# A two-layer GLA and differential-attention trunk: channel-major activations, contiguous weight tiles, and one head of the next unit ahead of an out-projection

## The chip, the cores and the metric

The kernel runs on one core of one Trainium2 chip. A core has a matmul engine (TensorE, "PE" in the profile, with its weight loads as "PEld"), a vector engine (VectorE, "DVE"), an activation engine (ScalarE, "ACT"), GpSimd ("POOL") and a queue that issues DMAs (SyncE, "SP"). The metric is the device time of one execution in microseconds, lower is better; the time given is the median of several executions.

## The reference

The reference runs two layers over a sequence of 2048 tokens with 1024 channels, all in float32:

```python
for l in range(2):
    mod = silu(c) @ w_ada[l] + b_ada[l]              # c: 1 x 1024
    shift, scale, gate = split(mod, 3)
    h = rms_norm(x, norm_g[l]) * (1 + scale) + shift
    proj = h @ w_in[l]                               # 1024 -> 3600 columns
    gq, gk, gv, glr, gz, dq, dk, dv, dz = split(proj)
    gq, gk, gv = silu(causal_conv4([gq, gk, gv]))    # then gated linear attention, 4 heads, chunks of 64
    o_gla  = rms_norm(gla(gq, gk, gv, glr)) * silu(gz)
    o_diff = rms_norm(softmax1 @ dv - lam * softmax2 @ dv) * silu(dz)   # 4 heads, block-causal in chunks of 64
    x = x + gate * ([o_gla, o_diff] @ w_out[l])
```

`rms_norm` divides each token by the root of its mean square over channels. The result is `x` after the second layer.

## The kernel before

**Tiling.** The sequence is cut into four units of 512 tokens; with two layers there are eight units, which I number 0 to 7 (0 to 3 are layer 0). A unit's normalised input h is held channel-major, as eight tiles k of 128 channels by 512 tokens, each twice: `hhi` is h rounded to the matmul's fast float32 form, `hlo` the remainder. A weight tile is split likewise, into `hi` and `lo`. A product then takes three matmuls of 512 moving columns (hi·hi, lo·hi, hi·lo), accumulated over the eight k in one PSUM bank.

**Items of a unit.** The input projection is done as seven items of 512 columns: items 0 to 3 are the attention heads (each with the head's q, k, v and z), items 4 and 5 are the columns of the gated linear attention (GLA), item 6 is its output gate gz. An item has 96 matmuls (8 k, 4 banks, 3 products). The out-projection (`out_gen`) has two halves of 96 matmuls. An item occupies four PSUM banks of the pool `acc`; the other four banks (`tp`, `sc`, `po`) serve everything else. In the profile's names, `acc<-w,hhi` and `acc<-w,hlo` are the matmuls of the heads and of the gate (token-major result), `acc<-hhi,w` those of the GLA items (channel-major result), `acc<-w,oh` and `acc<-w,ol` those of the out-projection (oh, ol are the two parts of its input, four k from GLA and four from the heads).

**Making h.** For layer 0, unit 0 this is `start()`; otherwise `prep_gen`. `load_x` (line 703) loads 128 tokens by 1024 channels as `xt`, takes the sum of squares on ACT, the root on POOL, and scales the tile on DVE. `make_h` (line 719) turns it channel-major on PE: 8 transposes of 128x128 for each 128 tokens, 32 in a unit (`sc<-ident,xt`, `tp<-ident,xt`), then ACT applies the scale and shift out of PSUM and writes `hhi`, and DVE writes `hlo`. The buffers of `hhi` and `hlo` are single, so tile k of the next unit can only be written when the last matmul of the current unit (item 6) has read tile k.

**Modulation.** In layer 0, shift and scale come from `ada_load` and `ada_first` (lines 573 and 580): 8 MB of w_ada are loaded and multiplied on PE (`tp<-wr,cact`, then `sc<-sel,t`). The gate of the residual is computed in `ada_part` part 2, broadcast over tokens by a matmul with ones, and multiplied into the raw w_out tiles on DVE (line 679) before these are split.

**Weights.** `weights` (line 667) loads a raw tile on first use, splits it on ACT and DVE, and writes the split tile to DRAM (`wd`); later units load the split tile. For item 0 of layer 0 the split is done in units 0 and 1 and kept in unit 1 only.

**Order of the work.** Streams of generators (projections, attention, GLA, preparation, modulation) are merged by a list of due times; each operation is recorded, and a planner (`Program.order`, `best_order`, lines 215 and 248) lists the operations with its own costs and fixes each engine's order before the kernel runs. On the chip every engine goes through its list in order and waits where an operand isn't there. `dense_stream` (line 1317) is the stream of the projections: for each unit it waits for h, then takes the out-projection of the unit before, then the unit's items. The exception is the first unit of layer 1, where two heads come ahead of the out-projection:

```python
ahead = 2 if l and u == 0 else 0
if ahead:
    yield from dense_gen(l, u, items[:ahead])
if prev:
    yield from out_gen(*prev)
yield from dense_gen(l, u, items[ahead:])
```

All DMAs are issued by SP, in its list's order.

## Time and profile before

| | |
|---|---|
| time, median of 3 runs | 2454.96 us (2453.43 to 2455.94) |
| the profiled execution's own time | 2454.26 us |
| its span, first to last instruction | 2452.5 us |
| PE busy | 2403.7 us (98%), 13251 matmul records |
| DVE busy | 1778.8 us (73%) |
| ACT busy | 1283.8 us (52%) |
| DMA, share of 16 engines | 71.5%, 568.33 MB |
| granted PE clock | 1.000 |

The span is 1.8 us shorter than the execution's own time, and that time lies 0.7 us under the median. A busy time is the union of the instructions' spans; a matmul's span includes its pipeline, so that the next one starts before it ends, and the distance from start to start is what a matmul costs in a row of them. A float32 matmul that isn't in the fast form is two records in the trace. Almost all instructions are recorded by one helper and so share line 372; groups are told apart by the names of their tiles.

### The profile page before, as it was taken

How to read it: one execution, taken by the hardware profiler on the slowest of the kernel's cores; microseconds unless marked ns; L12 is line 12 of the kernel's file. 1: busy time of each engine (PE TensorE's matmuls, PEld its weight loads, DVE VectorE, ACT ScalarE, POOL GpSimd, SP SyncE). 2: the span in 40 equal slices, each digit the busy share in tenths (PEclk: the TensorE clock that was granted, in tenths of full speed). 3: DMA queues.
4: the chain of work that ended last, by engine and by line, in shares of the span. 5: the costliest groups of instructions: out<-in, count | busy, mean ns of one | idle time of the engine just before them, and what ended most of it. 6: DMA issues, size and time to landing. Idle time of an engine off the chain costs nothing. (4 is left out here: it accounts for less than half of the span.)

```text
span 2452.5 us, 39647 instructions
## 1 busy us (share of the span) xinstructions
PE 2403.7 (98%) x13251; PEld 1957.3 (80%) x13251; DVE 1778.8 (73%) x5169; ACT 1283.8 (52%) x2912; POOL 138.2 (6%) x424
## 2 busy tenths in 40 slices
PE   8999999999999999999999999999999999999998
PEld 5887778888888877888788777888788887878887
DVE  4879778882879828889764894778648877288983
ACT  5757545572555624455863573455624556145442
POOL 0101000010000000000000010000000000000000
PEclk9999999999999999999999999999999999999999
DMA  9778988667786776778467867676667776677663
GB/s 275 274 252 281 328 260 252 216 234 235 224 253 190 256 230 189 220 216 248 140 221 262 298 246 271 212 235 202 212 234 224 232 232 215 223 223 225 196 200 131
DMA packets 425997, 568.33 MB, mean 232 GB/s; under 512 B 195968, under 2 KB 300608, under 8 KB 425792
## 3 DMA queue, kind: packets, MB, share of 16 engines
q1 hardware_dynamic: 425792, 565.79, 71.5%
q8 instruction: 105, 1.72, 0.3%
q14 instruction: 100, 0.82, 0.1%
HBM read 410.52 MB, written 161.48 MB: 233 GB/s over the span
## 5 line engine op out<-in xcount | busy, mean ns | idle before, releaser
L372 PE MATMUL acc<-w,hhi 128*128 128x512 f32 x2560 | 835.0, 400 | 3.7 <-DVE z L372 1.2
L372 PEld LDWEIGHTS acc<-w,hhi 128*128 128x128 f32 x2560 | 467.8, 188 | 97.9 <-ACT ub L372 3.9
L372 PE MATMUL acc<-w,hlo 128*128 128x512 f32 x1280 | 505.9, 396 | 0.0
L372 ACT ACTIVATE s<-s,mx 128x128 f32<-128x128 f32 (+15 forms) x256 | 308.2, 1204 | 263.3 <-DVE s L372 151.2
L372 PE MATMUL acc<-hhi,w 128*128 128x512 f32 x1024 | 353.6, 399 | 0.0
L372 PE MATMUL acc<-w,oh 128*128 128x512 f32 x1024 | 334.0, 399 | 4.7 <-DVE t L372 2.2
L372 DVE TENSOR_SCALAR_CACHE_REDUCE s<-sc,mx 64x64 f32<-64x64 f32 (+5 forms) x640 | 306.4, 483 | 37.5 <-PE sc L372 18.2
L372 PEld LDWEIGHTS acc<-w,hlo 128*128 128x128 f32 x1280 | 240.7, 188 | 48.8 <-issue 0.8
L372 PEld LDWEIGHTS acc<-w,oh 128*128 128x128 f32 x1024 | 188.9, 188 | 46.1 <-DVE t L372 5.2
L372 PEld LDWEIGHTS acc<-hhi,w 128*128 128x128 f32 x1024 | 191.8, 188 | 38.5 <-DMA w<-wd 0.7
L372 PEld LDWEIGHTS po<-Vj,s 128*128 128x128 f32 x1536 | 193.4, 196 | 12.4 <-DMA s<-ad 5.7
L372 PE MATMUL po<-Vj,s 128*128 128x128 f32 x1536 | 198.9, 281 | 3.7 <-DMA s<-ad 2.5
L372 PE MATMUL acc<-w,ol 128*128 128x512 f32 x512 | 201.5, 396 | 0.0
L372 PE MATMUL acc<-hlo,w 128*128 128x512 f32 x512 | 201.0, 393 | 0.0
L372 DVE SCALAR_TENSOR_TENSOR s<-s,r 128x512 f32<-128x512 f32 (+2 forms) x320 | 198.4, 667 | 2.6
L372 DVE TENSOR_SCALAR_CACHE_REDUCE s<-sc 128x512 f32<-128x512 f32 (+4 forms) x256 | 157.8, 620 | 39.9 <-PE sc L372 31.5
L372 ACT COPY rw<-acc 128x256 f32<-128x256 f32 x128 | 48.4, 378 | 252.7 <-PE acc L372 252.1
L372 PE MATMUL sc<-Kj,qh 128*128 128x512 f32 x384 | 160.3, 417 | 4.1 <-DVE z L372 2.2
L372 POOL MEMSET s<- 64x64 f32 x256 | 37.2, 145 | 2086.1 <-PE po L372 1505.5
L372 DVE TENSOR_TENSOR w<-raw,w 128x512 fp32r<-128x512 f32 x152 | 103.3, 686 | 67.7 <-ACT w L372 67.0
L372 PE MATMUL sc<-Kj,ql 128*128 128x512 f32 x384 | 151.7, 395 | 0.0
L372 ACT CAST w<-raw 128x512 fp32r<-128x512 f32 x152 | 93.3, 628 | 102.9 <-PE acc L372 90.6
(185 smaller groups left out, 3738.6 us busy)
## 6 DMA issues: line engine op xcount, KB each, us to landing
w<-wd SPq DMA_DIRECT2D x424, 512.0 KB, 4.6
wd<-w SPq DMA_DIRECT2D x144, 512.0 KB, 4.0
raw<-in_w_in_dram SPq DMA_DIRECT2D x120, 256.0 KB, 4.7
Kj<-kd SPq DMA_DIRECT2D x48, 512.0 KB, 5.8
ad<-s SPq DMA_DIRECT2D x24, 768.0 KB, 5.3
s<-ad SPq DMA_DIRECT2D x24, 768.0 KB, 7.4
wr<-in_w_ada_dram SPq DMA_DIRECT2D x128, 128.0 KB, 3.0
ad<-s SPq DMA_DIRECT2D x32, 512.0 KB, 3.7
```

Source lines behind the costliest of these rows:

```text
L372: getattr(self.engines[e], method)(*[real(a) for a in args], **{k: real(v) for k, v in kw.items()})
```

## The change

**Layouts.** The host hands the arrays over in other layouts: x channel-major per unit (`xl`: unit, 128 channels of a tile, 8 tiles, 512 tokens) and also as it was; the nine weight items of each layer as contiguous tiles of two k each (`w_all`); the columns for glr, the small vectors, the lambdas and w_gk each in one array; the shift and scale columns of layer 0's w_ada transposed (`w_mod`). The result is written channel-major and turned on the host; the intermediate x (`XD`) is channel-major too.

**h.** `make_h` now takes a channel-major x tile: DVE multiplies it by the channel's scale and by the tokens' reciprocal roots (broadcast over partitions, `rsb`), ACT adds the shift and writes `hhi`, DVE writes `hlo`. There is no transpose of x. The reciprocal roots go through a small DRAM row (`RD`) and are broadcast by a DMA. Their sums of squares come, for units 1 to 3, from a second load of x token-major (ACT); for layer 1 from squares added up in `out_gen` (ACT and DVE) and four matmuls with a ones column (`sc<-ones,sqs`); for unit 0 in the same way inside `start()`.

**Start.** `start()` computes shift and scale of layer 0 per k on DVE (`wm<-wm,cb` with an accumulated sum) and no longer on PE. Items 0 and 4 of unit 0 run together: for each k, as soon as h of that k is there, both items' matmuls of that k, in the four `acc` banks and in the four other banks. The raw tiles of item 4 are therefore, like those of item 0, split twice (units 0 and 1) and kept in unit 1.

**Out-projection.** Weights are the stationary and oh, ol the moving operand, so that the result is channel-major; the gate is one scalar per channel and is applied when the bank is added to x (`scalar_tensor_tensor` in place of `tensor_tensor`). The multiplication of raw w_out by the gate goes.

**Order.** In all units but the first of layer 1, the first item (head 0) of a unit is put ahead of the previous unit's out-projection (`ahead` is 1 instead of 0); unit 0 takes the same item order as the others.

```diff
-    def make_h(l, xs, pr, kk):
+    def make_h(l, k, xk, rsb):
         y = layers[l]
-        ps = tp() if kk % 2 else sc()
-        for j in range(2):
-            k = 2 * kk + j
-            for i in range(2):
-                T.transpose(ps[:, j * 256 + i * P:j * 256 + i * P + P], xs[i][:, k * P:(k + 1) * P], ident)
...
+        hi, lo = state["hhi"][k], state["hlo"][k]
+        V.scalar_tensor_tensor(xk, xk, y.A[:, k:k + 1], rsb, op0=ALU.mult, op1=ALU.mult)
+        A.activation(hi, xk, AF.Identity, bias=y.B[:, k:k + 1])
+        V.scalar_tensor_tensor(lo, xk, y.B[:, k:k + 1], hi.bitcast(F32), op0=ALU.add, op1=ALU.subtract)
+
+    def add_square(sqs, xk, first):
+        if first:
+            A.activation(sqs, xk, AF.Square)
+        else:
+            sq = t2()
+            A.activation(sq, xk, AF.Square)
+            V.tensor_tensor(sqs, sq, sqs, op=ALU.add)
+
+    def sum_squares(sqs):
+        ps = sc()
+        for t in range(TT):
+            T.matmul(ps[:, 2 * t:2 * t + 1], sqs[:, t * P:(t + 1) * P], ones[:, 0:1], start=True, stop=True)
+        return ps[:, 0:2 * TT].rearrange("p (t o) -> p t o", o=2)[:, :, 0]
...
     def prep_gen(l, u, xsrc):
         key = l * NU + u
+        if l == 0:
+            yield need("h", key - 1, lag=6.0)
+            ss = p_sm.tile([P, TT], F32, tag="xss", name="xss", bufs=2)
+            for t in range(TT):
+                xt = p_q.tile([P, D], F32, tag="q", name="xt")
+                SY.dma_start(xt, x[u * UT + t * P:u * UT + (t + 1) * P, :])
+                A.activation(xt, xt, AF.Square, accum_out=ss[:, t:t + 1])
+                yield pe(0, 2.0)
+            rs_write(key, root(ss))
+        rsb = rs_tile()
+        SY.dma_start(rsb, RD[key].broadcast_to([P, UT]))
         yield need("free_h", key)
...
+        for c in range(KT // 2):
+            xp = p_q.tile([P, 2, UT], F32, tag="q", name="xp")
+            SY.dma_start(xp, xsrc(u)[:, 2 * c:2 * c + 2, :])
+            for j in range(2):
+                make_h(l, 2 * c + j, xp[:, j, :], rsb)
...
     def start():
...
+        for k in range(KT):
...
+            for part in range(2):
+                V.scalar_tensor_tensor(wm[k][:, part, :], wm[k][:, part, :], 0.5, cb, op0=ALU.mult, op1=ALU.mult,
+                                       accum_out=sv[:, part:part + 1])
...
+            make_h(0, k, xs[k // 2][:, k % 2, :], rsb)
+            for it, ring in zip(FIRST, (acc, sc)):
+                hi, lo = weights(0, 0, it, k)
+                if k == 0:
+                    first_banks[it] = [ring() for _ in range(4)]
+                for j in range(4):
+                    (mm3T if it >= 4 else mm3N)(first_banks[it][j], k, slice(j * P, (j + 1) * P), hi, lo)
...
-                    mm3(banks[t], oh[:, ts_], ol[:, ts_], hi, lo, n_ == 0, n_ == KT - 1)
+                    T.matmul(banks[j], hi[:, js], oh, start=(n_ == 0), stop=False)
+                    T.matmul(banks[j], hi[:, js], ol, start=False, stop=False)
+                    T.matmul(banks[j], lo[:, js], oh, start=False, stop=(n_ == KT - 1))
...
-                V.tensor_tensor(rt[:, t, :], banks[t], rt[:, t, :], op=ALU.add)
+                V.scalar_tensor_tensor(rt[:, j, :], banks[j], y.gate[:, d:d + 1], rt[:, j, :], op0=ALU.mult, op1=ALU.add)
...
-                items = (0, 1, 4, 5, 2, 3, 6) if u == 0 else order
-                ahead = 2 if l and u == 0 else 0
+                items = order if u or not l else (0, 1, 4, 5, 2, 3, 6)
+                ahead = 2 if l and u == 0 else 1
```

Three places of the planned order follow, each first before and then after the change. The first is the beginning of PE's list. `tp<-wr` and `sc<-sel` are the modulation, `xt` the transposes of x, `sqs` the sums of squares, `tp<-t,ones` the broadcast of the roots.

```order
L372 MATMUL tp<-ident,crow 128x8
L372 MATMUL tp<-wr_119,cact_166 32x256 x8
L372 MATMUL tp<-wr_130,cact_166 32x256 x8
L372 MATMUL tp<-ident,t_140 128x128
L372 MATMUL sc<-ident,xt 128x128 x5
L372 MATMUL sc<-sel,t_234 128x1 x4
L372 MATMUL sc<-ident,xt 128x128 x3
```

```order
L375 MATMUL sc<-ones,sqs 128x1 x4
L375 MATMUL tp<-t_230,ones 128x128 x4
L375 MATMUL acc<-w,hhi 128x512 x5
L375 MATMUL acc<-w,hlo 128x512 x2
L375 MATMUL acc<-w,hhi 128x512
```

After the change eight small matmuls stand ahead of the first projection matmul, and no modulation and no transpose is mixed with the projections behind it; from there the list goes on with item 0 and item 4 in turn.

The second place is on PE between the last matmul of unit 0's item 6 (the first two rows of each piece) and the next big group: `z` and `s` are transposes of the attention, `po` its products with V, `vN` the transposes of the GLA output.

```order
L372 MATMUL acc<-w,hhi 128x512 x2
L372 MATMUL acc<-w,hlo 128x512
L372 MATMUL acc<-w,oh 128x512 x2
L372 MATMUL acc<-w,ol 128x512
L372 MATMUL acc<-w,oh 128x512 x2
L372 MATMUL acc<-w,ol 128x512
L372 MATMUL tp<-ident,s 128x128 x3
L372 MATMUL acc<-w,oh 128x512
L372 MATMUL sc<-ident,xt 128x128
```

```order
L375 MATMUL acc<-w,hhi 128x512 x2
L375 MATMUL acc<-w,hlo 128x512
L375 MATMUL tp<-ident,z 128x128 x2
L375 MATMUL acc<-w,hhi 128x512 x2
L375 MATMUL tp<-ident,s 128x128 x4
L375 MATMUL po<-Vt,s 128x128 x4
L375 MATMUL tp<-ident,z 128x128
L375 MATMUL tp<-ident,vN 128x128 x2
L375 MATMUL acc<-w,hhi 128x512
L375 MATMUL tp<-ident,z 128x128
L375 MATMUL tp<-ident,vN 128x128 x7
```

Before, the out-projection (`oh`, `ol`) stood there. After, come the first four matmuls of unit 1's head 0 on h tile 0, then the rest of the transposes, then (not shown) one `acc`, seven more `vN`, the sixteen glr matmuls that read all of unit 1's h, and only then the rest of head 0; the out-projection comes behind head 0.

The third place is DVE at the same moment, about the middle of the stretch in which the next unit's `hlo` are written. `t<-t,acc` is the gate's SiLU, `vN<-vN,gw,t` its product with the GLA output, `ol` the out-projection's input, `am` the modulation sums for later.

```order
L372 SCALAR_TENSOR_TENSOR ol<-tp,dg_645,oh 128x512
L372 TENSOR_TENSOR w<-raw,w 128x512
L372 TENSOR_TENSOR hlo<-t_3190,hhi 128x256 x2
L372 SCALAR_TENSOR_TENSOR ol<-tp,gg_642,oh 128x512
L372 SCALAR_TENSOR_TENSOR am<-wr,cact,am 128x256
```

```order
L375 SCALAR_TENSOR_TENSOR ol<-tp,dg_149,oh 128x512
L375 SCALAR_TENSOR_TENSOR vN<-vN,gw,t_2887 128x128 x4
L375 SCALAR_TENSOR_TENSOR xp<-xp,A_225,rsb 128x512 x2
L375 SCALAR_TENSOR_TENSOR am<-wr,cact,am 128x256
L375 SCALAR_TENSOR_TENSOR ol<-tp,gg_147,oh 128x512
L375 SCALAR_TENSOR_TENSOR hlo<-xp,B_215,hhi 128x512 x2
```

The h tiles now take two operations of 512 columns each on DVE (`xp` and `hlo`), where they took two `hlo` of 256 columns and a share of the `xt` scaling, and they stand between the same gate products.

## The prediction

> **What bounds the kernel now.** I read the page first, then the groups by shape on PE and DVE, then windows and the order of time at two places, the start and the border between units.

> ```profile
> span 2452.5 us, 39647 instructions
> PE 2403.7 (98%) x13251; PEld 1957.3 (80%) x13251; DVE 1778.8 (73%) x5169; ACT 1283.8 (52%) x2912; POOL 138.2 (6%) x424
> ```

> PE is idle for 2452.5 - 2403.7 = 48.8 us in all, so the time can change by what PE executes and by what is added to or taken from these waits; other engines matter only where PE waits for them. A busy sum of overlapping matmuls doesn't give their price. That is read from starts in the order of time:

> ```profile
> 257.42 0.61 PE L372 MATMUL acc<-w,oh 128*128 128x512 f32 x2
> 257.87 0.39 PE L372 MATMUL acc<-w,ol 128*128 128x512 f32 x1
> 258.10 0.61 PE L372 MATMUL acc<-w,oh 128*128 128x512 f32 x2
> 258.58 0.63 PE L372 MATMUL sc<-ident,xt 128*128 128x128 f32 x4
> 259.04 0.60 PE L372 MATMUL tp<-ident,xt 128*128 128x128 f32 x4
> 259.48 0.60 PE L372 MATMUL sc<-ident,xt 128*128 128x128 f32 x4
> 259.91 0.60 PE L372 MATMUL tp<-ident,xt 128*128 128x128 f32 x4
> 260.27 0.47 PE L372 MATMUL acc<-w,ol 128*128 128x512 f32 x1
> ```

> Three matmuls of 512 columns take 258.10 - 257.42 = 0.68, so 0.227 us each and 5.4 us for the 24 of two items and one k. The sixteen transposes take 260.27 - 258.58 = 1.69, so 0.106 each. The projections and the out-projection keep their number; swapping the out-projection's operands changes neither columns nor weight loads (front: 3 x 128x512 either way), so I price it at nothing.

> **Term 1, the transposes of x.**

> ```profile
> L372 PE MATMUL sc<-ident,xt 128*128 128x128 f32 x128 | 22.0, 285 | 2.0 <-DVE xss L372 2.0
> L372 PE MATMUL tp<-ident,xt 128*128 128x128 f32 x128 | 20.8, 278 | 0.3 <-DVE s L372 0.3
> ```

> All 256 go; 32 of them belong to the start, term 2. The other 224 at 0.106 give **-23.7 us**. They run on the engine that has no slack, so I take the whole of it; bounds 0 (if they only filled waits, a rival) and -28.

> [...]

> **Term 2, the start.** Here PE waits for x, for the modulation and for the first weights.

> ```profile
> 0.00:5.00 5.00, 0.24 (x1) 0.18 (x1) 2.38 (x23) 2.12 (x3) 1.09 (x8) 1.00 0.54 164
> 5.00:10.00 5.00, 2.32 (x20) 0.89 (x24) 0.00 (x0) 0.00 (x0) 0.00 (x0) 1.00 1.09 367
> 10.00:15.00 5.00, 2.47 (x18) 0.76 (x10) 1.71 (x5) 3.45 (x6) 1.11 (x2) 1.00 1.06 383
> 0.00:80.00 80.00, 67.66 (x400) 46.76 (x401) 44.54 (x152) 47.25 (x101) 4.03 (x17) 1.00 0.86 267
> 0.00:60.00 60.00, 7.01 (x32) 1.00 0.92 277
> L372 PE MATMUL tp<-wr,cact 128*32 128x256 f32 x128 | 11.0, 465 | 5.1 <-DMA wr<-in_w_ada_dram 5.1
> L372 PE MATMUL sc<-sel,t 128*128 128x1 f32 x32 | 4.7, 267 | 0.1
> 6.72 1.94 PE L372 MATMUL tp<-wr,cact 128*32 128x256 f32 x16 [4.09 <-DMA wr<-in_w_ada_dram]
> 17.21 1.83 PE L372 MATMUL sc<-sel,t 128*128 128x1 f32 x8
> 23.80 1.07 PE L372 MATMUL tp<-wr,cact 128*32 128x256 f32 x16
> 26.97 0.95 PE L372 MATMUL sc<-sel,t 128*128 128x1 f32 x8
> ```

> (The window's first column behind the length is PE; the fifth row counts the transposes of x alone.) In the first 80 us PE is idle for 80 - 67.66 = 12.3, and does work that vanishes: 11.0 for the modulation, 4.7 for its turning, 7.0 for 32 transposes. These spans overlap the next instruction's by some 0.16 at each change of group; I take 19 of their 22.7. Dead time of the start before: 31 us.

> After: vectors, c (0.5 MB broadcast), x (2.1), one w_mod tile (1.05) and two raw tiles (1.05) are issued in this order. The rows show 367 and 383 GB/s once loads flow, from about 2.4 us on. At 375, x is there at 2.4 + 2.7/0.375 = 9.6. Behind it stand a square (0.6 on ACT), its sum (0.6 DVE), four small matmuls (1.8, as at 17.21), the root on POOL, the diagonal and its four matmuls (together some 4), the copy (0.6), `xp` (0.7) and `hhi` (0.7), and a hop of 0.1 to 0.2 between each: the first projection matmul starts at about 20 us. From there PE has 24 matmuls per k, 5.4 us; DVE has two sums of 1024 columns (1.2 each, twice the 0.60 of 512), `xp`, `hlo`, two splits and three small ones, 2.4 + 1.3 + 1.2 + 0.3 = 5.2; DMA has 1.57 MB, 4.3 at 367. PE is just the slowest, so the two items end near 20 + 8 x 5.4 = 63, plus 1 for stumbles between two nearly equal engines. And the first matmuls run slow: the same sixteen take 1.94 at 6.72 and 1.07 at 23.80. I charge 2. Dead time after: 20 + 1 + 2 = 23, gain **-8**; bounds 0 (DVE sets the pace with instruction spans instead of distances, 6 per k) and -12 (root and diagonal overlap the loads).

> **Term 3, added PE work.** Four sums of squares in units 0 to 3 as at 26.97, 4 x 0.95 = 3.8. The gate's modulation becomes 32 records of the small kind (0.95/8 each, 3.8) in place of 16 broadcast records:

> ```profile
> L372 PE MATMUL sc<-am,ones 128*128 128x256 f32 x16 | 5.1, 403 | 0.0
> ```

> These come in pairs whose tails overlap, so half of 5.1 goes. Together **+5**, bounds 3 and 6.

> **Term 4, the borders.** Before, the out-projection (42 us) stood between item 6 and the next unit's first head, and h was made meanwhile. Now head 0 follows item 6. What h takes, at the border to unit 1 (rows: h alone, then DVE in order of time):

> ```profile
> 242.00:267.00 25.00, 3.11 (x8) 0.86 (x8) 6.04 (x16) 5.88 (x16) 1.00 0.78 272
> 242.00:267.00 25.00, 24.93 (x135) 19.47 (x135) 24.71 (x62) 21.21 (x51) 2.18 (x4) 1.00 0.78 272
> 246.42 0.68 DVE L372 SCALAR_TENSOR_TENSOR t<-t,acc 128x512 f32<-128x512 f32 x1
> 247.02 0.47 DVE L372 SCALAR_TENSOR_TENSOR am<-wr,cact,am 128x256 f32<-128x256 f32 x1
> 247.42 1.13 DVE L372 SCALAR_TENSOR_TENSOR vN<-vN,gw,t 128x128 f32<-128x128 f32 x4
> 248.48 0.76 DVE L372 TENSOR_TENSOR hlo<-t,hhi 128x256 fp32r<-128x256 f32 x2
> 249.16 0.48 DVE L372 SCALAR_TENSOR_TENSOR am<-wr,cact,am 128x256 f32<-128x256 f32 x1
> 249.55 0.74 DVE L372 SCALAR_TENSOR_TENSOR ol<-tp,dg,oh 128x512 fp32r<-128x512 f32 x1
> 250.22 0.68 DVE L372 TENSOR_TENSOR w<-raw,w 128x512 fp32r<-128x512 f32 x1
> ```

> DVE is full there (24.71 of 25 us), and PE was too, with other work. In the changed order DVE has, from the gate's first SiLU to unit 1's last `hlo`: 4 SiLU x 0.60, 16 `vN` x 0.26, 6 `xp`, 7 `hlo`, 3 `ol` and 1 `s` x 0.66, 3 `am` x 0.40, 2 `z` x 0.26, 0.1, after a tanh of 0.6: 20.2 us from the moment the gate's first bank is done. PE then has the 18 matmuls left of item 6 (4.1), 24 transposes and four `po` x 0.106 and four `acc` (another 3.9), and the sixteen glr matmuls (3.7), which go in step with h: 11.7 us. PE stands 20.2 - 11.7 = 8.5 us. Border n is the one into unit n. Counted in the same way, PE's cover against DVE up to the first use of h tile 4 is, for borders 2 to 7: 20 against 15, 20 against 23, 23 against 15, 18 against 14, 19 against 13, 20 against 23; two more stalls of 3. What PE already loses near these three:

> ```profile
> 236.00:300.00 64.00, 62.69 (x316) 48.84 (x315) 53.69 (x121) 40.64 (x85) 3.11 (x8) 1.00 0.92 325
> 820.00:900.00 80.00, 75.95 (x403) 60.03 (x402) 49.87 (x134) 41.08 (x87) 5.16 (x14) 1.00 0.75 238
> 2030.00:2110.00 80.00, 77.01 (x404) 61.14 (x403) 44.28 (x113) 37.94 (x81) 5.17 (x14) 1.00 0.75 243
> ```

> 1.3, 4.1 and 3.0 us, which the new order replaces. So 8.5 + 3 + 3 - 8.4 = +6, and 1 for hops: **+7**, bounds -7 (all covered) and +35 (second rival).

> [...]

> **What costs nothing.** Gone from DVE and off PE's path: 32 gate products and the `xt` scaling; added: squares, a second split of item 4. DVE at 73% hides them outside the borders. DMA gains 6 MB of x read again, and the roots' 2 KB through DRAM; if that cover failed it would show as PE waiting for `w`. The new wait on SP is the load of `rsb` behind the write of `RD`, of the kind that is there for the attention blocks:

> ```profile
> SPq L372 <- DMA ad<-s: 70.2, 41, 6.2
> ```

> At most 6.2 us; queued behind it are weight loads, and four `w` buffers hold 4 x 12 x 0.227 = 10.9 us of matmuls.

> **Sum.** 2454.3 (the profiled execution's own time; the median of the runs is 0.7 above) - 23.7 - 8 + 5 + 7 = 2434.6. I forecast **2434 us**, own range 2424 to 2444.

> **Rivals.** (a) *The borders are covered*: the planner finds enough attention work, and the old waits go too; term 4 at -7 gives 2420. For it: five of seven borders have cover in my count. Against: DVE full at border 1. (b) *Slower, h is late at every border.* Written in the old tempo, h's tiles spread over 25, 29, 35, 37, 22, 29 and 36 us (the stretches in which the sixteen writes of `hhi` lie; the first is in a row above, the longest and the last here):

> ```profile
> 1165.00:1202.00 37.00, 7.90 (x22) 4.03 (x23) 6.02 (x16) 5.80 (x16) 1.00 0.29 101
> 2031.00:2067.00 36.00, 3.12 (x8) 0.86 (x8) 6.04 (x16) 5.81 (x16) 1.00 0.78 253
> ```

> The changed order has 8, 24, 26, 27, 16, 23 and 26 us of PE work from item 6's end to the last glr matmul. The differences sum to 63, less some 16 of idle that is there already: +47 instead of +7, 2475. It decides from a net 27 us on the borders. Against: `xp` can run before the tiles are free, and the gate products and weight splits that stood between the h tiles on DVE no longer do (third place of the order). (c) *The transposes were filler*: they stand in windows where DVE is full, so what goes is waited instead; term 1 at -8 gives 2450. (d) *The start is paced by DVE*: term 2 at 0, 2442. [...]

> **How the numbers follow.** Forecast 0.45, (a) 0.22, (b) 0.08, (c) 0.12, (d) 0.10, (e) 0.03. 0.2% of the time, about what a measurement tells from no change, is 4.9 us. Faster than 2450: forecast, (a), (d), (e) and half of (c), 0.86 less a little for mishaps, 0.85; same 0.07; slower 0.08. The range 2411 to 2450 leaves out (b), (e) and a tail of (a) and (c).

> **What would show it.** PE without `xt` records; first `acc` matmul near 20 us and 192 of them done by 66; a PE gap of 5 to 10 us ahead of the glr matmuls of unit 1, released by DVE `hlo`, and small ones in units 3 and 7; PE idle in all about 50 us. Wrong if the gaps at the borders exceed 27 us together, or if PE's waits elsewhere grow by what the transposes took.

## The result, and the profile after

The changed kernel is slower: 2475.62 us (median of 4 runs, 2473.18 to 2479.16) against 2455.45 of the kernel before on the same chips; the ratio is 1.0083, with a 95% interval of 1.0065 to 1.0100. The forecast was 2434, range 2411 to 2450. The profiled execution took 2479.16, the longest of the four.

The head of the page after with its clock row, and in the second fence the two halves of the span, layer 0 up to about 1200 us and layer 1 behind it, of the change (columns: window, length, then PE, PEld, DVE, ACT, POOL busy with counts, granted clock, DMA share, GB/s):

```profile
span 2477.2 us, 38561 instructions
PE 2388.0 (96%) x12896; PEld 1944.8 (79%) x12896; DVE 1827.2 (74%) x5158; ACT 1240.6 (50%) x2726; POOL 123.2 (5%) x400
...
PEclk9899899999999999999999999999999999999999
```

```profile
0.00:1200.00 1200.00, 1128.41 (x6014) 911.94 (x6015) 915.95 (x2582) 613.16 (x1348) 63.39 (x198) 0.98 0.75 240
1200.00:2400.00 1200.00, 1190.75 (x6507) 974.80 (x6506) 877.12 (x2492) 603.47 (x1333) 57.26 (x195) 1.00 0.71 230
```

and of the kernel before:

```profile
0.00:1200.00 1200.00, 1169.12 (x6489) 946.26 (x6489) 906.81 (x2664) 654.25 (x1488) 71.28 (x219) 1.00 0.75 240
1200.00:2400.00 1200.00, 1189.10 (x6519) 973.48 (x6518) 855.80 (x2468) 618.80 (x1402) 65.28 (x203) 1.00 0.70 228
```

PE is idle for 2477.2 - 2388.0 = 89.2 us where it was idle for 48.8. All of the 40 more lie in the first 1200 us (71.6 idle against 30.9); the second half didn't change (9.3 against 10.9). DVE isn't much busier in that first half, 916 against 907: the loss is one of order and lateness, not of DVE's total.

PE's busy time fell by only 15.7 us, and the clock row says why: in the second and the fifth slice it falls to 8, and shorter stretches don't show at this width. In windows around three of the places, each time the 3.41 us ahead and then the stretch itself:

```profile
85.13:88.55 3.42, 0.79 (x3) 0.19 (x1) 3.35 (x6) 3.40 (x7) 0.00 (x0) 1.00 0.00 0
88.55:98.79 10.24, 8.24 (x28) 5.09 (x29) 8.55 (x25) 8.09 (x18) 0.00 (x0) 0.50 0.50 183
600.55:603.96 3.41, 0.96 (x4) 0.82 (x5) 0.00 (x0) 0.61 (x2) 0.00 (x0) 1.00 1.03 410
603.96:607.37 3.41, 3.41 (x10) 2.63 (x9) 2.81 (x6) 0.00 (x0) 0.00 (x0) 0.50 0.93 380
996.50:999.91 3.41, 0.00 (x0) 0.00 (x0) 0.00 (x0) 0.00 (x0) 0.00 (x0) 1.00 0.57 83
999.91:1006.74 6.83, 5.73 (x14) 4.36 (x15) 0.75 (x1) 0.69 (x1) 0.00 (x0) 0.50 0.90 364
```

Nine stretches of 3.4 to 10.2 us, 51 us in all, run at a granted clock of 0.50: in 603.96 to 607.37 PE gets ten matmuls done where fifteen of 0.227 would go. The kernel before has no such stretch in its profiled execution before its last instruction; its other executions show a granted clock of 0.998 to 1.000. Its emptiest window after the start in its trace, and the one behind it, which isn't slow:

```profile
1186.48:1189.89 3.41, 1.86 (x15) 1.65 (x16) 3.35 (x11) 2.65 (x4) 1.04 (x2) 1.00 0.30 116
1189.89:1193.30 3.41, 2.74 (x23) 2.26 (x22) 1.04 (x7) 3.41 (x7) 0.00 (x0) 1.00 0.00 0
```

The balance is worked out from the starts of all PE records (distance to the next start, less the idle time before it): PE's work was 2403.3 us before and is 2387.6 after. In run e1 below, with a granted clock of 0.998 over the run, the same matmuls took 2407.3 less 43.8 of added zeros, 2363.5. So the work fell by 40 (the forecast said 36), the half clock took 24 of it back, and 40 us more idle time make the span longer: -40 + 24 + 40 = +24, and the spans differ by 24.7. (PE was busy for 45.5 us in the slow stretches, and half of that, 22.7, is a second estimate of what they took. e1 itself still has 10 us at half clock, so the split is good to some 5 us.)

What PE waits for, the longest rows of the view of waits (total, times, longest), after:

```profile
PE acc L375 <- DMA w<-wd: 15.5, 5, 6.2
PE sc L375 <- DVE sqs L375: 14.7, 1, 14.7
PE sc L375 <- DVE s L375: 7.0, 9, 1.5
PE tp L375 <- DVE s L375: 4.2, 8, 2.2
...
PE sc L375 <- DVE am L375: 3.2, 3, 1.3
PE tp L375 <- DVE rw L375: 3.0, 1, 3.0
```

The list before begins with 5.1 us for `wr`, all at the start, and nothing else reaches 4. New are the split weights that come late (15.5 us, at 386, 603, 674 and 1001 us, where the kernel before waits 1.3) and a row of DVE waits in unit 0 (80 to 125 us) and around the border to unit 1 (236 to 320 us):

```profile
0.00:80.00 80.00, 60.46 (x259) 48.50 (x260) 70.76 (x188) 38.80 (x74) 3.29 (x14) 1.00 0.80 296
80.00:125.00 45.00, 34.93 (x147) 25.68 (x146) 33.93 (x106) 32.41 (x83) 3.62 (x11) 0.82 0.44 144
236.00:320.00 84.00, 72.47 (x314) 51.93 (x314) 63.87 (x172) 50.02 (x102) 3.60 (x9) 0.92 0.82 260
```

19.5, 10.1 and 11.5 us idle; from 80 to 125 us neither DVE nor ACT is full on average and the DMA engines are 44% busy, so a chain of hops between the engines is likely; it isn't shown, and at PE's first long gap there (85.13 to 88.55 above) DVE and ACT are both full. As idle time there is hardly a wait for h at the borders, where the forecast had put it. The two groups that read h first, over all eight units:

```profile
L375 PE MATMUL sc<-hhi,wglr 128*32 128x512 f32 x64 | 27.0, 422 | 1.7 <-DVE ol L375 1.7
L375 PE MATMUL sc<-hlo,wglr 128*32 128x512 f32 x64 | 26.6, 415 | 0.1
```

These rows hide one wait, though. At the borders to units 2 to 7 the sixteen glr matmuls of a unit take 3.9 us and never stand. At the border to unit 1 they take 6.9, from 256.97 to 263.85, with most of it at half clock, and the last of them starts at 263.43, just after DVE has written the last `hlo` (263.38). So h sets their pace there: besides the 1.7 us ahead of them some 3 us of waiting for h are filled by the slow clock and count as busy.

The largest single gap around that border comes later and looks like this, in DVE's order of time and then in PE's:

```profile
285.85 1.01 DVE L375 SCALAR_TENSOR_TENSOR am<-wr,cact,am 128x256 f32<-128x256 f32 x2 [5.81 <-DMA wr<-in_w_ada_dram]
...
291.86 1.00 DVE L375 SCALAR_TENSOR_TENSOR am<-wr,cact,am 128x256 f32<-128x256 f32 x2 [4.25 <-DMA wr<-in_w_ada_dram]
...
299.05 0.18 DVE L375 SCALAR_TENSOR_TENSOR rq<-nb,rq 128x16 f32<-128x16 f32 x1
302.36 0.48 DVE L375 SCALAR_TENSOR_TENSOR am<-wr,cact,am 128x256 f32<-128x256 f32 x1 [3.13 <-DMA wr<-in_w_ada_dram]
...
304.75 1.43 DVE L375 TENSOR_TENSOR rw<-rw,rq 128x256 f32<-128x256 f32 x4
```

```profile
301.88 0.39 PE L375 MATMUL acc<-oh,w 128*128 128x512 f32 x1
305.23 0.66 PE L375 MATMUL tp<-ident,rw 128*128 128x128 f32 x2 [2.96 <-DVE rw L375]
```

DVE is in the middle of head 0's root (`nb`, `rq`) when its list has a step of layer 1's modulation, whose piece of w_ada isn't there: 3.1 us of standing, and PE, which needs `rw`, stands 2.96. Late loads reach PE by this way too, not only by `w`.

The late weights themselves, SP's issues ahead of the waits at 603 and 1001 us (the second column is how long the issue itself took):

```profile
586.85 0.37 SPq L375 DMA_DIRECT2D rd<-xrs  x1
...
595.68 0.32 SPq L375 DMA_DIRECT2D rsb<-rd  x1
596.10 0.86 SPq L375 DMA_DIRECT2D w<-wd  x2
```

```profile
975.73 5.39 SPq L375 DMA_DIRECT2D xd<-rt  x1
...
982.47 5.49 SPq L375 DMA_DIRECT2D Vj<-vp  x1
988.06 0.39 SPq L375 DMA_DIRECT2D rd<-xrs  x1
988.54 0.93 SPq L375 DMA_DIRECT2D w<-wd  x2
```

At 591 SP stands for 4.9 us at the broadcast of the roots, which waits for their write, and the weights stand behind it: the wait that the forecast had found and let pass. Ahead of 1001 two issues take 5.4 and 5.5 us; the second, of a load of V, names no semaphore that it could wait for. Long issues are not new: the change has 21 of over 2 us, the kernel before 20. What is new comes behind: the load of `w` that PE waits for at 1001 is issued at 988.54, right after the write of the roots (`rd`), and lands at 1000.96, 12.4 us later, where 4.5 is the median. In such places the DMA engines are taken up and move next to nothing (last two columns):

```profile
664.00:666.00 2.00, 2.00 (x12) 1.64 (x11) 0.00 (x0) 0.00 (x0) 0.00 (x0) 1.00 0.81 20
992.00:996.00 4.00, 2.79 (x22) 2.35 (x21) 0.29 (x1) 0.66 (x3) 0.69 (x2) 1.00 1.02 39
```

The write of the roots is 2 KB in 512 pieces of 4 bytes, and there are seven of them. In the change a packet of 4 KB takes 0.19 us on average, but 0.56, and up to 6.5, from 2 to 10 us behind such a write. Stretches of 2 us with a DMA share over 0.8 and less than 100 GB/s (counted in steps of 2 us from 30 to 2440) exist in all fourteen kernels of this case that have these writes, 102 together, each beginning within 11 us behind one (in the change seven, behind five of its seven writes), and in none of the five that don't (the kernel before, e6, e11, e12, e15). The load behind the wait at 674 was issued 4.8 us behind a write and took 9.5 us; the pieces of w_ada that DVE stands for until 285.8 were issued 3.4 us behind one and took 10.9, where 3.9 is the median. So the small writes stand ahead of most of the late loads. No run takes them out, so what they cost is not shown.

### The profile page after: what moved, and what is told of

It reads as the page before. It is cut to its first block, busy times and chain, and to the rows that moved or that the text cites. A ratio compares the mean times of both kernels' runs of the same rounds, so it can differ in the third digit from the quotient of the medians.

```text
span 2477.2 us, 38561 instructions
## 1 busy us (share of the span) xinstructions
PE 2388.0 (96%) x12896; PEld 1944.8 (79%) x12896; DVE 1827.2 (74%) x5158; ACT 1240.6 (50%) x2726; POOL 123.2 (5%) x400
## 3 DMA queue, kind: packets, MB, share of 16 engines
q1 hardware_dynamic: 372968, 571.32, 71.6%
## 4 chain that ended last, share of the span: by engine, by line
PE 71%; DVE 15%; DMA 7%; ACT 4%; issue 2%; SPq 1%; POOL 0%; POOLq 0%; DVEq 0%; ACTq 0%
PE acc L375 47%; PE sc L375 11%; PE po L375 9%; DVE s L375 6%; PE tp L375 4%; DMA wr<-in_w_ada_dram 3%; DMA w<-wd 2%; DVE t L375 1%; DVE w L375 1%; DVE am L375 1%; ACT s L375 1%; SPq L375 1%; ACT qh L375 1%; DMA s<-ad 1%; DVE hlo L375 1%
## 5 line engine op out<-in xcount | busy, mean ns | idle before, releaser
L375 ACT ACTIVATE s<-s,mx 128x512 f32<-128x512 f32 (+15 forms) x256 | 308.3, 1204 | 308.8 <-DVE s L375 162.7
L375 PE MATMUL acc<-oh,w 128*128 128x512 f32 x1024 | 358.7, 402 | 6.7 <-DMA w<-wd 3.6
L375 PE MATMUL acc<-hhi,w 128*128 128x512 f32 x960 | 323.4, 402 | 10.7 <-DMA w<-wd 9.5
L375 PEld LDWEIGHTS acc<-oh,w 128*128 128x128 f32 x1024 | 193.0, 189 | 50.3 <-DMA w<-wd 4.0
L375 PEld LDWEIGHTS acc<-hhi,w 128*128 128x128 f32 x960 | 181.5, 190 | 49.7 <-DMA w<-wd 11.1
L375 PE MATMUL acc<-ol,w 128*128 128x512 f32 x512 | 202.2, 395 | 0.0
L375 PE MATMUL acc<-hlo,w 128*128 128x512 f32 x480 | 190.4, 397 | 0.0
L375 DVE TENSOR_TENSOR w<-raw,w 128x512 fp32r<-128x512 f32 x160 | 108.9, 686 | 53.5 <-ACT w L375 52.7
L375 DVE SCALAR_TENSOR_TENSOR t<-ub,vec,t 128x512 f32<-128x512 f32 x192 | 138.3, 747 | 5.6 <-ACT t L375 5.1
```

Of the source, the lines that this page charges most:

```text
L375: getattr(self.engines[e], method)(*[real(a) for a in args], **{k: real(v) for k, v in kw.items()})
```

## The experiments

Each run's ratio is against runs of the kernel before on its own chip, whose median goes from 2453.9 to 2456.6 over the chips; differences of medians in the text aren't corrected for that. "Idle" is span less PE busy and "half clock" the length of the stretches at 0.50 (without one in the last 3 us), both in the profiled execution. "Order kept" means that the edit comes after the planner, so that every engine's list is that of the changed kernel; in the others the planner made a new order. e5, e14 and e16 leave a part of the computation out.

| run | edit | median (range), us | ratio, 95% | idle | half clock |
|---|---|---|---|---|---|
| change | | 2475.6 (2473.2-2479.2) | 1.0083, 1.0065-1.0100 | 89.2 | 51 |
| e1 | zeros in the gaps, order kept | 2469.8 (2465.3-2474.5) | 1.0053, 1.0037-1.0069 | 55.7 | 10 |
| e2 | roots issued by POOL, order kept | 2477.6 (2473.4-2478.7) | 1.0081, 1.0066-1.0096 | 85.4 | 55 |
| e3 | one first item | 2470.0 (2469.3-2473.2) | 1.0056, 1.0041-1.0071 | 87.4 | 44 |
| e4 | old order at the borders | 2506.3 (2505.0-2512.8) | 1.0210, 1.0192-1.0228 | 109.5 | 65 |
| e5 | second x load small, order kept | 2470.9 (2465.0-2472.3) | 1.0062, 1.0047-1.0077 | 85.7 | 44 |
| e6 | before, with the new order | 2490.5 (2488.1-2492.7) | 1.0143, 1.0126-1.0160 | 67.8 | 31 |
| e7 | another seed | 2470.3 (2465.2-2477.7) | 1.0066, 1.0046-1.0087 | 86.8 | 38 |
| e8 | e3 with zeros | 2475.3 (2471.3-2478.0) | 1.0083, 1.0068-1.0098 | 60.6 | 20 |
| e9 | h's product on POOL | 2475.8 (2468.6-2477.8) | 1.0078, 1.0057-1.0098 | 92.7 | 48 |
| e10 | and the sums of squares | 2472.1 (2470.9-2475.5) | 1.0071, 1.0056-1.0086 | 92.6 | 38 |
| e11 | before, another seed | 2457.0 (2455.6-2463.0) | 1.0014, 1.0005-1.0024 | 51.4 | 10 |
| e12 | before, hlo twice, order kept | 2496.1 (2493.4-2497.6) | 1.0165, 1.0150-1.0180 | 73.8 | 10 |
| e13 | third wr buffer, order kept | 2470.5 (2468.3-2474.5) | 1.0062, 1.0047-1.0077 | 83.3 | 44 |
| e14 | e1, e2, e5, e13 at once | 2464.3 (2463.9-2468.7) | 1.0043, 1.0029-1.0057 | 56.0 | 14 |
| e15 | before, with the new start | 2455.7 (2451.5-2459.1) | 1.0000, 0.9991-1.0009 | 63.9 | 14 |
| e16 | e14 with fewer zeros | 2458.5 (2453.6-2465.3) | 1.0020, 1.0011-1.0029 | 64.0 | 17 |
| e17 | e16, x loads in full | 2464.2 (2456.1-2472.4) | 1.0038, 1.0022-1.0053 | 71.2 | 31 |

**e1: is the half clock the loss?** Matmuls of zeros are put ahead of 24 waiting matmuls; they leave the results of these as they are. `FILL` names instructions by number and gives how many matmuls of zeros go ahead of each.

```diff
+    FILL = {575: 15, 588: 4, ..., 7832: 36, ..., 19268: 4}
+    def fill(self, i, method, args, kw, real):
...
+        for _ in range(self.FILL.get(i, 0)):
+            self.engines["T"].matmul(o, self.zero[:, 0:p], self.zero[:, 0:n], start=first, stop=first)
```

> The changed kernel, every engine's order kept, with 276 extra matmuls of zeros put ahead of 24 waiting instructions of PE (the 24 gaps before or inside the half-clock stretches, and the other gaps over 1.2 us); they add nothing to the sums. Theory CLOCK: the changed kernel ran 51 us (nine stretches of 3.4 to 10.2 us) at a granted clock of 0.5, and each stretch begins after a 3.4-us window in which PE stood idle for 1.2 to 3.4 us. PE is the bound, so a stretch loses half its length: with the gaps filled no clock of 0.5 is left after 30 us, PE's real work takes some 22 us less, and the time is 2455 (2450 to 2462). Theory STALLS: the waits themselves are the loss and the slow stretches stand where PE would wait anyhow; the clock may rise, but the time stays within 5 us of 2476.

```profile
PE 2407.7 (98%) x13172; PEld 1976.9 (80%) x13172; DVE 1827.5 (74%) x5159; ACT 1240.7 (50%) x2726; POOL 123.1 (5%) x400
...
PEclk9999999999999999999999999999999999999999
```

The clock came back, and 44 us of extra matmuls made the kernel faster, not slower: 5.8 us in the median (the traces compare the slowest of the change's four executions with the fastest of e1's). CLOCK is right about the cause of the slow matmuls (24 us of PE's work) and wrong about the price. The gain that reaches the end is a quarter of it, since zeros and idle time together are 43.8 + 55.7 = 99.5 us where 89.2 were idle: PE arrives earlier and waits longer. Between the theories, nearer STALLS.

**e2: SP's queue.** At issue, the 14 root transfers go to POOL's queue instead of SP's.

```diff
+            if e == "S" and ... args[0].buf.name[:2] in ("rd", "rs"):
+                e = "G"
             getattr(self.engines[e], method)(...)
```

> The changed kernel with the same order, only the 14 transfers of the reciprocal roots (7 writes to the DRAM row, in 4-byte pieces, and 7 broadcasts back) are issued by POOL, which is 5% busy, instead of SP. Theory QUEUE: the weight loads were late because SP stood in line at those transfers (4.9 us at 591 and 9.3 us at most behind a write, 5.6 us for a root at 982). Then PE's waits for w at 386, 603, 674 and 1001 (15 us together) and the half-clock stretches behind three of them (13.7 us, half of it lost) go: 2476 - 15 - 7 = 2454 (2450 to 2462). Theory TRAFFIC: the loads are late because the DMA engines are busy (72%, and 512 pieces of 4 bytes in a write); then the waits for w stay whoever issues, and the time is 2476 within 5.

Half of each. PE's waits for `w` fell from 15.5 to 5.3 us, so QUEUE was right about most of those. But a load of the attention (`s`) that took 13.8 us to land now stops PE for 3.5 us at 994: the writes in pieces of 4 bytes are still there whoever issues them, so this run doesn't rule TRAFFIC out. And the wait at the broadcast only moved: POOL now stood at the broadcast, and with it the small root that DVE and PE need in unit 0. POOL's order of time, then PE's:

```profile
111.13 0.93 POOL L377 DMA_DIRECT2D rd<-xrs  x1 [0.17 <-POOL s L377]
...
120.93 0.60 POOL L377 DMA_DIRECT2D rsb<-rd  x1 [6.05 <-DMA rd<-xrs]
121.55 0.59 POOL L377 TENSOR_TENSOR wq<-oss,mhalf 128x1 f32<-128x1 f32 x1
```

```profile
122.58 0.69 PE L377 MATMUL tp<-ident,z 128*128 128x128 f32 x2 [3.78 <-DVE z L377]
```

Compared matmul by matmul with the change's trace, e2 loses 5 us up to 120 us and wins 11 later; the median shows no gain.

**e3, e8: two first items.**

```diff
-    FIRST = (0, 4)
+    FIRST = (0,)
-                items = order if u or not l else (0, 1, 4, 5, 2, 3, 6)
+                items = order if u else (0, 1, 4, 5, 2, 3, 6)
```

> The changed kernel with one first item instead of two together, and unit 0 in the old item order (0, 1, 4, 5, 2, 3, 6); the planner makes a new order. Theory UNIT0: two items at once put 8 us more of DVE work (evacuations of both) on the stretch from 50 to 125 us, where DVE was busy 45 of 50 us; PE's waits at 88 to 119 (9.4 us) and the 17 us at half clock behind them (8.5 lost) come from it and go. Against that the start loses: per k one item is 2.7 us of PE against some 4.5 us of DVE, so 8 x 1.8 = 14 us. Net 2473 (2465 to 2482), with the waits at 88 to 119 gone and the start's idle time up by 14. Rival: the waits in unit 0 stay (they belong to GLA and attention work of a unit without a past) and the start loses as well: 2490.

```profile
0.00:80.00 80.00, 55.62 (x228) 41.68 (x229) 68.29 (x190) 44.61 (x85) 3.29 (x14) 0.96 0.80 305
80.00:125.00 45.00, 42.34 (x219) 34.51 (x218) 37.47 (x134) 35.59 (x108) 6.91 (x22) 1.00 0.88 263
236.00:320.00 84.00, 69.48 (x312) 51.39 (x311) 62.28 (x166) 48.96 (x99) 3.18 (x7) 0.90 0.83 258
```

As UNIT0 said: from 80 to 125 us idle time falls from 10.1 to 2.7 and the half clock goes, up to 80 us it grows from 19.5 to 24.4. Net 5.6 us, and the border to unit 1 loses 3 more. With zeros in its gaps as in e1, this kernel should have gained again:

> The kernel of the run with one first item (2470), its order kept, with 269 matmuls of zeros ahead of 19 waiting instructions of PE (the gaps before and inside its stretches at half clock, 41 us, and those over 1.2 us). The sums stay as they are. By the first run with zeros, where 51 us at half clock became 10 and the time fell by 6 in the median and 14 in the profiled execution: 41 us x 6/41 to 14/41, 2464 to 2456, faster than the kernel before only if all of it comes back. If the waits alone are the loss: 2470.

It lost 5 instead, although half clock went from 44 to 20 us: 48 us of zeros and 60.6 of idle time stand where 87.4 were idle. So holding the clock alone is no reliable gain; the six of e1 and the minus five of e8 are of the size by which orders differ (e7).

**e4, e6: the order at the borders.** In the change back to the old, in the kernel before to the new:

```diff
-                ahead = 2 if l and u == 0 else 1
+                ahead = 2 if l and u == 0 else 0
```

> The changed kernel with the order of before at the borders: the out-projection of a unit ahead of all items of the next (the first unit of layer 1 keeps its two items ahead); the planner makes a new order. Theory ORDER: head 0 ahead of the out-projection leaves h too little cover; what PE lost from 246 to 305 us (8.0 us of gaps over 0.9 us, 13.6 us at half clock) and at later borders goes away: 2476 - 8 - 7 = 2461 or less. Rival, the order helps: without it h and the weights of the first item meet at the border and the time grows above 2485.

> The kernel before with one edit: head 0 of a unit ahead of the previous unit's out-projection, in all units but the first of layer 1 (unit 0 keeps its items); the planner makes a new order. Theory COVER: the out-projection was the cover under which the old kernel made h in 25 to 37 us; without it PE waits at each border by what the second rival counted (differences of 5 to 13 us, 47 in all), and some 3.4-us windows fall to half clock: 2456 + 47 = 2503 (2485 to 2515). Theory ORDER: head 0 first is worth something by itself (the changed kernel loses 30 us without it), then it is faster here too: 2440 to 2450.

e4 is 31 us slower than the change, e6 36 us slower than the kernel before. Neither order is better by itself: the new one belongs to the new h and the old one to the old. My theory ORDER fell; COVER gave the right sign, with 36 where its sum gave 47, but the profile of e6 has no single long wait at a border: idle time grew by 19 in pieces of at most 2.1 us after the start, and 31 us run at half clock.

**e5: the second load of x.** Order kept; 8 of 1024 columns are loaded and squared.

```diff
+            if ... args[0].buf.name == "xt":
+                args = [v[:, 0:8] ...]
```

> The changed kernel with the same order; the 12 loads of x token-major for the sums of squares of units 1 to 3 (512 KB each) and their squares on ACT take 8 of 1024 columns, so that the roots of layer 0's units 1 to 3 are those of 8 channels (this part of the computation is left out). Theory TRAFFIC: these 6 MB, which no unit of layer 1 loads, make the weight loads late in units 1 to 3; the waits for w at 386, 603, 674 and 1001 (15 us) and the half-clock stretches behind three of them (13.7 us, half of it lost) go: 2476 - 15 - 7 = 2454 (2450 to 2462). Theory ISSUE: the loads are late because SP is held at transfers that stay (5.4 us at the write of x and 5.5 us at a load of V ahead of the wait at 1001, the write of the roots and the broadcast behind it ahead of that at 603); then the waits stay and the time is 2476 within 4.

Between: the wait at 386 us is gone and that at 674 down to 0.9, those at 603 (3.8) and 1001 (5.8) stay, and 5 us are gained. TRAFFIC explains two of the four.

**e7, e11: the order as chance.**

```diff
-        ops, rnd = self.ops, random.Random(0)
+        ops, rnd = self.ops, random.Random(1)
```

> The changed kernel with another seed of the planner's search and nothing else: how much of a difference is the order found by chance. If the loss belongs to the change, the time is 2470 to 2482, with a wait for h at the border to unit 1 and for w in units 1 to 3 again. If it belongs to one unlucky order, it falls below 2465, or rises above 2485.

> The kernel before with another seed of the planner's search and nothing else, beside the changed kernel with another seed (2470 against 2476). If the kernel before is one lucky order, it loses 8 us or more: above 2463. If the difference belongs to the change: 2450 to 2460.

Another order moves the change by -5 and the kernel before by +2.5; e7 has the same picture again (`w` late at 590, 665 and 994 us, 86.8 idle). The loss belongs to the change, and by these two pairs a single new order can't be read closer than some 5 us: e3, e9 and e10 are no gains by this measure.

**e9, e10, e12: DVE's work.** In units 1 to 7, POOL multiplies x by the roots; in e10 POOL also adds the squares in the out-projections.

```diff
+        if l or key:
+            G.tensor_tensor(xk, xk, rsb, op=ALU.mult)
+            A.activation(xk, xk, AF.Identity, scale=y.A[:, k:k + 1], bias=y.B[:, k:k + 1])
+            A.copy(hi, xk)
+            V.tensor_tensor(lo, xk, hi.bitcast(F32), op=ALU.subtract)
+            return
```

> The changed kernel with the product of x and the roots moved from DVE to POOL in units 1 to 7 (56 tiles of 128x512; ACT then applies scale and shift, copies hhi, and DVE has only the difference); the planner makes a new order. Theory DVE: the change put 48 us more on DVE (1779 to 1827), and at the borders, in eight stretches of 70 to 110 us that hold them, DVE's share went from 65 to 82%; PE's new waits at 246 to 305 us and part of those behind it are DVE's. With 45 us taken off DVE at these places they shrink: 2476 - 8 (waits) - 7 (half clock) - some of the rest = 2455 (2445 to 2463), DVE busy 1782. Rival, LATENCY: h is a chain of hops and POOL's product takes longer than DVE's 0.75 us; then h comes later and the time is 2476 or more.

> As the run with the product on POOL, and the sums of squares in the out-projections of layer 0 (28 additions of 0.68 us) on POOL too: DVE another 19 us less, 1763. Theory DVE: a little faster than that run, by 2 to 8 us. Rival: these additions lay in places where DVE had time, no difference within 4 us.

Neither gained beyond chance. DVE's busy time fell by 15, not by 45: other instructions of it took longer on average, `s<-s,r` 681 ns in place of 667, `r<-r,nlam,ls` 249 in place of 217, `vN` above all 412 in place of 346 (change, then e9). The 17 of the 128 `vN` that overlap a product on POOL took 869 ns on average, the other 111 took 342:

```profile
L375 DVE SCALAR_TENSOR_TENSOR vN<-vN,gw,t 128x128 f32<-128x128 f32 x128 | 37.1, 346 | 0.2
```

```profile
L375 DVE SCALAR_TENSOR_TENSOR vN<-vN,gw,t 128x128 f32<-128x128 f32 x128 | 46.9, 412 | 0.3
L375 POOL TENSOR_TENSOR xp<-xp,rsb 128x512 f32<-128x512 f32 x56 | 77.8, 1407 | 89.6 <-DMA xp<-in_xl_dram 43.8 <-DMA xp<-xd 36.3 <-DVE s L375 8.8
```

The mirror image is e12, the kernel before with every write of `hlo` issued twice:

```diff
+            if e == "V" and ... args[0].buf.name == "hlo":
+                getattr(self.engines[e], method)(...)
             getattr(self.engines[e], method)(...)
```

> The kernel before, order kept, with every write of hlo on DVE done twice (128 more of 0.42 us, the same numbers twice): 53 us more DVE work, as much as the change added, at the same places. Theory DVE: what is added to DVE at the borders is on PE's path: PE's idle time grows by 10 to 30 us, windows of 3.4 us fall to half clock, and the time is 2470 (2463 to 2490). Rival: DVE has time (73% busy) and h has cover: within 4 of 2455.

53 us of DVE work at these places cost 41.6 us, with DVE at 73%; theory DVE had the direction, and its range ended at 2490. So work at h isn't hidden by an average of 73%, not even in the kernel before. It doesn't follow that the change lost by it: its PE goes at the pace of `hlo` at one border only, and in e9, where the glr matmuls of that border take 3.8 us without a wait, the time is no better. That theory stays unproven for the change.

**e13, e14, e16, e17: the late loads and the clock together.** A third buffer for `wr`:

```diff
-        kw = {} if self.bufs is None else dict(bufs=self.bufs)
+        kw = {} if self.bufs is None else dict(bufs=3 if self.tag == "wr" else self.bufs)
```

> The changed kernel, order kept, with a third buffer for the pieces of w_ada (wr) that DVE multiplies for layer 1's modulation. In the trace of the change DVE stands 28.8 us at these loads (13.2 before), 5.8, 4.3 and 3.1 of it at 286, 292 and 302, right ahead of PE's waits at 293 and 305. Theory SIDE WORK: DVE works its list in order, and the side work's late loads hold up what PE needs: DVE's waits for wr fall below 15 us, PE's at 293 and 305 (4.2 us) go, and with their half-clock stretches the time falls by 5 to 10, to 2468. Theory QUEUE ORDER: these loads are late because SP comes to them late, whatever buffers there are: within 4 of 2476.

5 us faster, but not by the theory's sign: DVE still stands 27.1 us at these loads, the wait at 305 us stays (3.1); only the one at 293 is gone, and one of 1.0 has come at 287. Then everything at once:

> The changed kernel, order kept, with all of it at once: third wr buffer, the token-major x loads of units 1 to 3 cut to 8 of 1024 columns (the roots of layer 0's units 1 to 3 are those of 8 channels: this part of the computation is left out), the root transfers issued by POOL from unit 2 on, and 360 short matmuls of zeros in the 24 gaps. If waits for DMA (15 us) and half clock (24 us) are the loss and independent, it falls by both: 2476 - 39 = 2437, the forecast. If each only uncovers the next wait on the same chains of DVE and ACT, it falls by no more than the best of them alone did: 2465 to 2470.

2464.3, 11 below the change and more than any part alone, but far from 2437 and just under the range for uncovered waits. Its zeros took 42.2 us whether or not a wait was left to fill, so e16 has them only where DVE is late (19.1 us):

> As the run with everything at once, order kept, but with 154 short matmuls of zeros in place of 360: only in unit 0, at the border to unit 1 and in the last unit. In the run before this the zeros took 42 us of PE whether or not the wait they stood in was still there, so it could not show what the lighter DMA traffic is worth. (The roots of layer 0's units 1 to 3 are again those of 8 channels.) Theory SUM: the waits for w (15 us) have really gone, and without the zeros there PE runs on: 2464 - 15 = 2449, below the kernel before. Theory UNCOVER: other waits stand there, by DMA or DVE: 2460 to 2466.

```profile
PE 2387.8 (97%) x13050; PEld 1954.5 (80%) x13050; DVE 1825.8 (74%) x5159; ACT 1230.8 (50%) x2726; POOL 132.1 (5%) x412
...
PE acc L400 <- DMA w<-wd: 4.3, 4, 2.5
PE po L400 <- DMA s<-ad: 4.3, 2, 3.8
```

The median is 4.7 us above the kernel before on the same chip, where the change was 20.2 above. The profiled execution (span 2451.8), at the level of the kernel before, is the fastest of ten. The waits for `w` are 4.3 where they were 15.5, but those for `s` of the attention rose from 2.0 to 4.3. 2458.5 is 9.5 above SUM's 2449 and 1.5 under UNCOVER's range: nearer UNCOVER. With the second x load in full:

> The same with the token-major x loads in full, which computes everything. By SUM the difference between this and the last run is the price of the 6 MB of x: the run that cut them alone gave 5 us, so 2454 where the other is at 2449. By UNCOVER both are within 4 of each other and of 2464.

2464.2: the 6 MB cost about 6 us, as in e5; SUM had this difference right and the level wrong. Its wait at 375 us is now for a transfer of the attention (4.2 us). This version, which computes everything, is 10 us slower than the kernel before on its chip, half of the change's loss. None of these kernels beats it.

**e15: the start alone,** in the old kernel with old h, old out-projection, old order, one first item.

In words, since the edit is long: `small_vectors(True)`, `ada_load`, `ada_first` and the first `make_h` go, and `start()` of the change comes with `FIRST = (0,)` and with the weights as contiguous tiles.

> The kernel before with the new start alone: channel-major x for unit 0, modulation on DVE, weights as contiguous tiles, one first item; h by transposes, out-projection, order of the items as before. The planner makes a new order. Theory START GAINS: dead time 23 in place of 31 and 15 us of modulation work gone from PE: 2455 - 8 = 2447. Theory GIVEN BACK: unit 0 behind it is bound by its chains through DVE and ACT, PE only waits earlier or later: PE idle in the first 130 us grows by what its work falls, the time stays within 5 of 2455 or above.

```profile
PE 2393.4 (97%) x13072; PEld 1952.8 (79%) x13072; DVE 1802.3 (73%) x5203; ACT 1278.9 (52%) x2886; POOL 134.5 (5%) x421
...
0.00:80.00 80.00, 56.12 (x234) 42.46 (x234) 69.75 (x199) 42.62 (x85) 3.29 (x14) 0.98 0.74 280
```

Nothing gained, nothing lost (1.0000). PE's work fell by 10, its idle time grew by 15, 11.6 of it in the first 80 us. There 19.5 us lie ahead of the first projection matmul, and behind it PE waits 4.3 for h and `w` of one item (DVE is busy 69.75 of 80 us).

## Why the prediction was wrong

**Term 1 and term 3, the work: right.** 256 transposes cost 28.9 us by their starts before (0.113 each; 0.106 was used), and PE's whole work fell by 40 us at full clock. Rival (c), that they were filler, isn't needed for the work; that as much was waited elsewhere is told below. What rival (e) rests on no run shows: the 0.113 each is all that the trace has.

**Term 2, the start: the size a little off, the consequence missed.** The first matmul came at 23.5, not 20, and the 192nd ended at 69.0, not by 66. Dead time is 23.5 and about 2 for the slow first matmuls, against 31: -5.5 in place of -8. (The windows of before print a granted clock of 1.00 at the slow start. There is no record of the clock ahead of 22.5 us; see the last section.) But behind it unit 0 runs dry: from 80 to 125 us PE had been busy 44.9 of 45 us and now is 34.9, at a mean clock of 0.82. e3 moves that idle time back to the start, e15 shows the new start worth nothing in the old kernel. The gain is given back.

**Term 4, the borders: right at one place in kind, and not in form.** The gap of 8.5 us ahead of the glr matmuls of unit 1, released by `hlo`, isn't there: 1.7 us stand ahead of them, by `ol`, and some 3 more are hidden in their slow pace, which `hlo` does set. Units 3 and 7 have none. The stretch around the border to unit 1 (236 to 320 us) has 11.5 us of idle time; 4.2 of it in two gaps because DVE stood at loads of the side work and PE then waited for `am` and `rw`, which the term didn't have.

**"What costs nothing": the first failed step.** "Four `w` buffers hold 10.9 us of matmuls" was set against one wait of SP. In the trace it isn't one: the wait at the roots (4.9) and 6 MB more of loads come together, and above all the loads themselves are late, 9.5 and 12.4 us in place of 4.5, behind the roots' writes in pieces of 4 bytes. "The roots' 2 KB through DRAM" were counted as bytes and put at nothing. PE's waits for `w` rose to 15.5 us; e2, e5 and e16 each take part of them away. The sign named there ("PE waiting for `w`") is what came.

**The half clock: the second failed step.** The sum has no term for it, and it cost some 24 us of PE's work. The trace has six of its nine stretches at 0.50 behind gaps of 1 to 2.6 us, each after a window of 3.41 us with 1.2 us or more of idle time in all (below). Before, the emptiest window had 1.6 us of idle time, and in all runs every window with 2.1 or more was followed by half clock: the kernel stood just under that, and I read the granted clock of 1.00 as room.

**The sum.** For the span, 2432.8 was forecast: work 2367.6 and waits of about 65. The profiled execution has 2387.6 and 89. Work is off by +20 (the half clock's 24, less 4 for a little more work saved), waits by +24: 15.5 for `w`, 10 in unit 0, 3.5 at the start, and some 5 less elsewhere than forecast. These add up but aren't independent: e16, which takes most of the late loads and of the half clock away together and leaves the second x load out, gave 17 us, the parts alone 6 or less. What is left to the forecast, some 24 us, is mostly in unit 0 and at the border to unit 1 (most of e16's 19 us of zeros stand there), and no run removed those waits without others in their place. Why unit 0 runs dry stays open.

**Rival (b)** said 2475 and the time was 2475.6. That is chance: its mechanism, h late at every border by 47 us in all, was seen at one border with 3 to 5 us. Rival (d) holds for one first item (e15), not for two. What I said would show it wrong, gaps at the borders over 27 us together, didn't come; the other clause did, PE's waits elsewhere grew by what the transposes took.

## What to carry to other kernels

When an engine at 98% gets less work, ask of each place what it will wait for next, and above all which in-order queue stands there: a list that another engine works in order (DVE at side loads, SP at a write and its reader) turned one late transfer into a wait of the engine that needs something else (3.1 us of DVE at a piece of w_ada, and 2.96 of PE behind it). Look at how idle the emptiest 3.4-us windows of the matmul engine already are: here the emptiest had 1.6 us of idle time before, and the change, with 1.2 to 3.4 us in nine of them, paid for new gaps twice: 40 us more idle time, and some 24 us of PE's work at half clock. Count a transfer in pieces and not only in bytes: 2 KB in 512 pieces stand ahead of loads that took 9.5 and 12.4 us here in place of 4.5. And a forecast made of independent savings needs a test of the cover: doubling a cheap instruction at the place in question (53 us of DVE work cost 42) tells in one run what an average busy share hides.

## What the runs showed of the hardware

**Behind the roots' writes in 4-byte pieces transfers were slow.** In the fourteen kernels with the roots' writes, and in none of the five without, the DMA engines have stretches at under 100 GB/s with a share over 0.8, all within 11 us behind such a write; in the change a packet of 4 KB takes 0.56 us on average from 2 to 10 us behind one, in place of 0.19. No run tried the same bytes in larger pieces.

**Single issues took SP over 5 us.** In the change the issue of one load of V took 5.49 us and names no semaphore that it could wait for; 0.35 is the median. One write of x took 5.39, but there the view of waits has a wait for DVE's `xms`, which ended when the issue did. The kernel before has long issues too: 20 of over 2 us, three of which, of 5.1 to 6.8, name no semaphore.

**DVE's `vN` took longer beside POOL.** With 56 products of 128x512 on POOL (1.41 us each, e9) DVE's `vN` took 412 ns in place of 346 on average: 869 where it overlapped a product, 342 where not. `t<-t,acc`, which reads PSUM, took 680 beside a product and 681 otherwise. A third of what was to be taken off DVE was left as gain (15 of 45 us).

**With zeros in the gaps less ran at half clock.** In e1 two half-clock stretches were left where the change had nine (10 us of 51).
